# Dividing the gate of the heads' output, instead of the probabilities, by the softmax's row sums

## The chip, the cores and the metric

The program runs on one core of a Trainium2 chip. The metric is the device time of one execution in microseconds. A core has five engines with a queue of instructions each, which run in the order written: TensorE (PE in the profile), VectorE (DVE), ScalarE (ACT), GpSimd (POOL) and SyncE (SP, which only issues DMAs here). They wait for each other through semaphores. TensorE writes its results to PSUM, which the kernel divides into eight banks of 128 partitions by 512 fp32 values; VectorE and ScalarE read them there.

## The reference, cut to what matters

The model has two layers on 512 tokens with 16 learned meta tokens in front (528 rows, width 1024). The first layer mixes by attention with 16 heads of 64, the second by a gated delta net; after each stands a feed-forward block with a short convolution. Only the attention is touched by the change:

```
s = einsum('bhqd,bhkd->bhqk', q_i, k) * scale + c_i[..., :, None] - c[:, :, None, :]
p = softmax(where(mask, s, NEG), axis=-1)
o = einsum('bhqk,bhkd->bhqd', p, v)
o = o * sigmoid(og)
return (o @ w_out)[:, pad:]
```

`c` is the running sum of the log forget gates. The softmax divides each row of exponentials by its sum; the output of each head is then multiplied by a gate.

## The kernel before

Activations lie transposed, features on partitions and tokens along the free axis, in two halves of 272 and 256 tokens. Each fp32 product is made of three passes of rounded parts (hi by hi, hi by lo, lo by hi); `dense` (L312) does this for a weight tile of 1024x128 and one half of the tokens with 24 matmuls. A weight tile comes by DMA, ACT rounds it to its high part (L285), POOL or DVE subtracts to get the low part (L292); six tiles of each part take turns, so L285 waits until the tile used six units earlier has been read.

In attention the loop goes over eight pairs of heads. Each pair has four projections, q, k, v and the output gate og; for each, `push` lets the first half of the tokens run four units ahead of the second. `qk` normalizes q and k (L565 to L592), `vproj` flips v into rows of keys by transposes (L605, L610), and `og` computes the gate SG as exp(-log(1+exp(-z))) in three steps on ACT and one on POOL (L724 to L727), then calls `attend` for its half.

`attend` works on query blocks: 16, 128 and 128 queries in the first half, 128 and 128 in the second. For each block and each of the two heads, `scores` forms the scores in a PSUM bank `sc` (L646 to L649, of which there are two), DVE adds the forget sums and takes the row minimum (L650; signs are turned), ACT exponentiates with the row's sum as a by-product (L653), DVE takes the reciprocal of the sum and multiplies the whole row of probabilities by it (L654, L655). `flip` transposes the probabilities so that keys lie on partitions: first the 16 meta keys of both heads into a PSUM tile `pm` (L666), which ACT copies to PZ (L668) and DVE subtracts to get the low part (L669); then the other keys into tiles `pt` (L678), copied by ACT (L680) and subtracted by DVE (L681). `pm` and all `pt` tiles, those of `vproj` too, take turns in two PSUM banks: an instruction on PE that writes a new tile waits until the readers of the tile before last are done. `values` multiplies with v (L698), adds the parts (L699, L700), multiplies by the gate SG (L701) and rounds (L703, L704).

A flip lags one block behind the scores. The final order on each engine is not the order of the code: a scheduler with a timeline of its own interleaves the attention with the projections of the next pair, and raises those marked with a high priority. Any two instructions on different engines that use the same PSUM bank of one tile are put in order by it, reads included.

Of the kernel before, what the change touches and what calls it, by code (L numbers as in the profile page):

```python
# [9 lines left out]
F32 = mybir.dt.float32  # L10
F32R = mybir.dt.float32r
BF16 = mybir.dt.bfloat16
AF = mybir.ActivationFunctionType
ALU = mybir.AluOpType
# [3 lines left out]
P = 128  # L18
# [7 lines left out]
DH = 64  # L26
# [78 lines left out]
def trunk(ctx, tc, h0, wflat, params, out):  # L105
    nc = tc.nc
# [29 lines left out]
    def psum_tile(kind="ps"):  # L136
        rings = turn["kinds"][kind]
        i = turn.get(kind, 0)
        turn[kind] = i + 1
        ring = rings[i % len(rings)]  # L140
        return psp.tile([P, 512], F32, name=kind, tag=ring, bufs=BANKS[ring])
# [46 lines left out]
    ident = const.tile([P, P], F32, name="ident")  # L188
# [133 lines left out]
    def tmp2(name):  # L322
        return sm.tile([P, 272], F32, name=name, tag="tm2", bufs=5)
# [168 lines left out]
    def attention_heads(layer, OH, OL, cx):  # L492
        ap = cx.enter_context(tc.tile_pool(name="ap", bufs=1, reuse_waits="tile"))
# [15 lines left out]
        def persistent(name, tiles):  # L509
            ring[name] += 1  # L510
            return tiles[ring[name] % 2]
# [34 lines left out]
        for m in range(8):  # L546
            H = {}
# [71 lines left out]
            def attend(half, H=H, m=m):  # L619
                s, n = HALF[half]  # L620
                nkb = 2 if half == 0 else 4
                q0h = 16 if half == 0 else 272
                sfx = "A" if half == 0 else "B"
                Z = []
                PM = persistent("p", PZ)
                for e in range(2):
                    cB = ap.tile([P, s + n], F32, name="cB", tag=f"cB{half}", bufs=2)
                    nc.sync.dma_start(cB[:], cdram[2 * m + e:2 * m + e + 1, 0:s + n].to_broadcast([P, s + n]))
                    PTH = ap.tile([P, nkb, 256], F32R, name="PTH" + sfx, tag="PTH", bufs=2)
                    PTL = ap.tile([P, nkb, 256], F32R, name="PTL" + sfx, tag="PTL", bufs=2)  # L630
                    Z.append((cB, PTH, PTL))

                def scores(e, qb):
                    cB = Z[e][0]
                    QS, QL, KS = H["q", half, e], H["ql", half][e], H["k", e]
                    qs, ql = QB[qb]
                    ke = qs + ql
                    qc = slice(qs - s, qs - s + P)
                    S = ap.tile([P, T], F32, name="S", tag="S", bufs=4)
                    st = ap.tile([P, 4], F32, name="st", tag="st", bufs=6)  # L640
                    segs = ((0, ke),) if ke <= 512 else ((0, 264), (264, 264))
                    for i, (k0, kn) in enumerate(segs):
                        sc = psum_tile("sc")
                        lastseg = k0 + kn == ke
                        o = sc[:, 0:kn]
                        nc.tensor.matmul(o, QS[:, qc], KS[:, k0:k0 + kn], start=True, stop=False)  # L646
                        nc.tensor.matmul(o, QL[:, qc], KS[:, k0:k0 + kn], start=False, stop=not lastseg)
                        if lastseg:
                            nc.tensor.matmul(sc[:, kn - ql:kn], identb[:], cmask[:, :ql], start=False, stop=True)  # L649
                        nc.vector.tensor_tensor_reduce(out=S[:, k0:k0 + kn], in0=o, in1=cB[:, k0:k0 + kn], scale=1.0, scalar=3e38, op0=ALU.add, op1=ALU.min, accum_out=st[:, i:i + 1])  # L650
                    if len(segs) == 2:
                        nc.vector.tensor_tensor(st[:, 0:1], st[:, 0:1], st[:, 1:2], op=ALU.min)
                    nc.scalar.activation(S[:, 0:ke], S[:, 0:ke], AF.Exp, scale=-1.0, bias=st[:, 0:1], accum_out=st[:, 2:3])  # L653
                    nc.vector.reciprocal(st[:, 3:4], st[:, 2:3])  # L654
                    nc.vector.tensor_scalar(S[:, 0:ke], S[:, 0:ke], st[:, 3:4], None, op0=ALU.mult)  # L655
                    if qb == 0:
                        nc.gpsimd.memset(S[:, ke:P], 0.0)
                    return S

                def flip(qb, SS):  # L660
                    qs, ql = QB[qb]
                    qc = slice(qs - s, qs - s + ql)

                    pm = psum_tile("pt")
                    for e in range(2):
                        nc.tensor.transpose(pm[:, e * P:e * P + P], SS[e][:, 0:P], ident[:])  # L666
                    pv = pm[0:NM, 0:2 * P].rearrange("p (e q) -> p e q", e=2)[:, :, 0:ql]
                    nc.scalar.copy(PM[0:NM, :, qc], pv)  # L668
                    nc.vector.tensor_tensor(PM[32:32 + NM, :, qc], pv, PM[0:NM, :, qc].bitcast(F32), op=ALU.subtract)  # L669
                    if qb == 0:  # L670
                        return
                    x0 = qs - q0h
                    for e in range(2):
                        S = SS[e]
                        pt = pm[:, 256:512] if qb == 1 and e == 0 else psum_tile("pt")
                        PTH, PTL = Z[e][1:]
                        for kb in range(1, qb + 1):
                            nc.tensor.transpose(pt[:, (kb - 1) * 128:kb * 128], S[:, QB[kb][0]:QB[kb][0] + 128], ident[:])  # L678
                        pv = pt[:, 0:qb * 128].rearrange("p (k q) -> p k q", q=128)
                        nc.scalar.copy(PTH[:, 0:qb, x0:x0 + 128], pv)  # L680
                        nc.vector.tensor_tensor(PTL[:, 0:qb, x0:x0 + 128], pv, PTH[:, 0:qb, x0:x0 + 128].bitcast(F32), op=ALU.subtract)  # L681


                def values():
                    t = tmp2("avt")
                    w = tmp2("avw")
                    for e in range(2):
                        av = psum_tile("av")
                        PTH, PTL = Z[e][1:]
                        VV = H["v"]  # L690
                        es, eo = slice(64 * e, 64 * e + 64), slice(64 - 64 * e, 128 - 64 * e)
                        mm = [(av[:, 0:n], VV[:, 4, 2 * e:2 * e + 2], PM[:, e, 0:n])]
                        for ptx in (PTH, PTL):
                            for kb in range(1, nkb + 1):
                                lo = max(QB[kb][0], q0h)
                                mm.append((av[:, lo - s:n], VV[:, kb - 1, 2 * e:2 * e + 2], ptx[:, kb - 1, lo - q0h:256]))
                        for i, (o, l, r) in enumerate(mm):
                            nc.tensor.matmul(o, l, r, start=(i == 0), stop=(i == len(mm) - 1))  # L698
                        nc.scalar.copy(w[es, :n], av[eo, 0:n])  # L699
                        nc.vector.tensor_tensor(t[es, :n], av[es, 0:n], w[es, :n], op=ALU.add)  # L700
                    nc.vector.tensor_tensor(t[:, :n], t[:, :n], H["sg", half][:, :n], op=ALU.mult)  # L701
                    oh, ol = OH[half][:, m, :], OL[half][:, m, :]
                    nc.scalar.copy(oh, t[:, :n])  # L703
                    nc.vector.tensor_tensor(ol, t[:, :n], oh.bitcast(F32), op=ALU.subtract)  # L704

                prev = []
                for qb in ((0, 1, 2) if half == 0 else (3, 4)):
                    prev.append((qb, [scores(e, qb) for e in range(2)]))
                    if len(prev) > 1:
                        flip(*prev.pop(0))  # L710
                flip(*prev.pop(0))
                values()

            def og(u, half, H=H, m=m, attend=attend):
                n = HALF[half][1]
                xh, xl, r = xk(half)
                ps = dense(u, half, xh, xl)
                with tc.high_priority(offset=400):
                    z = tmp2("oz")[:, :n]
                    nc.vector.tensor_tensor(z, ps, r[:, :n], op=ALU.mult)  # L720
                    H["sg", half] = ap.tile([P, 272], F32, name="SG", tag="SG", bufs=2)
                    sg = H["sg", half][:, :n]

                    nc.scalar.activation(sg, z, AF.Exp, scale=-1.0)  # L724
                    nc.gpsimd.tensor_scalar(sg, sg, 1.0, 3e38, op0=ALU.add, op1=ALU.min)
                    nc.scalar.activation(sg, sg, AF.Ln)
                    nc.scalar.activation(sg, sg, AF.Exp, scale=-1.0)  # L727
                attend(half)
# [751 lines left out]
```

## Time and profile before

| | |
|---|---|
| median of 3 runs | 1603.53 us (1601.42 to 1608.82) |
| the profiled execution | 1601.35 us, span 1599.4 us |
| busy, share of the span | PE 95%, DVE 70%, ACT 51%, POOL 31% |
| granted TensorE clock | 0.977 in the mean, 1.00 in attention |
| instructions | 33295 |

A page of the profile gives the busy time of each engine, the longest waits and the chain of work that ended last; the trace behind it can be asked for stretches of time, lines and waits. A row of the order of time reads: start, duration, engine, line, operation, tile written and tiles read, shape, count, and in square brackets how long the engine stood idle before it and whose end released it. The durations of matmuls include their latency; successive matmuls overlap, so what one takes of PE is the distance between two starts. A row of stretches gives its length and the busy time of each engine with the number of instructions.

### The profile page before, as it was taken

The page shows a single profiled execution, that of the slowest core. Times are in us where ns is not written, and L with a number is a line of the kernel's source. Part 1 is how long each engine was busy: PE and PEld are TensorE (multiplying, and loading weights), DVE is VectorE, ACT ScalarE, POOL GpSimd, SP SyncE. Part 2 cuts the span into 40 slices and gives each one's busy share as a digit, 9 for nine tenths or more (in the row PEclk, how much of TensorE's full clock was granted, in tenths as well). Part 3 has the DMA queues.
Part 4 walks back from the last instruction along what each step waited for, and adds up shares of the span by engine and source line. Part 5 has one row for each costly group of instructions (what it writes and reads, how often), then busy time and mean ns, then how long its engine had stood idle before and what let it go on. Part 6 is the DMA issues. An engine that isn't in the chain of part 4 may idle for free.

```text
span 1599.4 us, 33295 instructions
## 1 busy us (share of the span) xinstructions
PE 1525.8 (95%) x12630; PEld 1486.8 (93%) x12630; DVE 1123.4 (70%) x2629; ACT 815.4 (51%) x1925; POOL 495.8 (31%) x993
## 2 busy tenths in 40 slices
PE   8999999999999999999789899899989999999996
PEld 6999999899999999999789798898989999999996
DVE  7888888948974675674978665676569864765764
ACT  6677777735643442343564456545456543432441
POOL 6434443025300010012556475654154200100112
PEclk9999999999999999999799998999999999999998
DMA  5232222422223222222323322222141323323321
GB/s 175 89 89 79 75 78 85 134 65 82 84 83 100 93 85 88 93 93 72 107 75 90 90 61 71 68 77 61 50 150 66 91 82 106 92 82 106 93 67 53
DMA packets 63327, 139.04 MB, mean 87 GB/s; under 512 B 18584, under 2 KB 31288, under 8 KB 62784
## 3 DMA queue, kind: packets, MB, share of 16 engines
q1 hardware_dynamic: 62544, 134.55, 28.1%
q8 instruction: 99, 1.62, 0.4%
q0 software_dynamic: 480, 2.15, 0.4%
q14 instruction: 60, 0.49, 0.1%
q10 hardware_dynamic: 144, 0.22, 0.0%
HBM read 131.54 MB, written 5.36 MB: 86 GB/s over the span
## 4 chain that ended last, share of the span: by engine, by line
PE 74%; DVE 11%; POOL 5%; DMA 4%; ACT 3%; issue 3%; SPq 1%; POOLq 0%; DVEq 0%; ACTq 0%
PE ps L312 65%; POOL PR L1177 2%; POOL RB L1178 2%; DVE h L412 1%; DVE bt L411 1%; DVE wl L292 1%; PE av L698 1%; DMA w<-wflat 1%; DVE cv L764 1%; DMA gcr<-gcd 1%; PE pt L678 1%; DVE xl L378 1%; ACT wh L285 1%; PE s L1277 1%; DVE qr L577 1%
## 5 line engine op out<-in xcount | busy, mean ns | idle before, releaser
L312 PE MATMUL ps<-xh,wh 128*128 128x256 f32 (+4 forms) x2464 | 717.6, 293 | 16.8 <-DVE ub L748 9.2
L312 PE MATMUL ps<-xl,wh 128*128 128x256 f32 (+4 forms) x2464 | 710.8, 289 | 3.4 <-DVE xl L378 3.0
L312 PE MATMUL ps<-xh,wl 128*128 128x256 f32 (+4 forms) x2464 | 713.6, 290 | 0.0
L312 PEld LDWEIGHTS ps<-xh,wh 128*128 128x128 f32 (+1 forms) x2464 | 469.6, 192 | 22.8 <-DVE ub L748 6.3
L312 PEld LDWEIGHTS ps<-xl,wh 128*128 128x128 f32 (+1 forms) x2464 | 471.1, 191 | 7.4 <-DVE xl L378 4.6
L312 PEld LDWEIGHTS ps<-xh,wl 128*128 128x128 f32 (+1 forms) x2464 | 471.1, 191 | 1.0
L285 ACT CAST wh<-w 128x1024 fp32r<-128x1024 f32 (+3 forms) x226 | 225.1, 997 | 189.5 <-PE ps L312 166.7
L292 DVE TENSOR_TENSOR wl<-w,wh 128x1024 fp32r<-128x1024 f32 (+4 forms) x191 | 220.6, 1156 | 99.3 <-ACT wh L285 98.7
L764 DVE SCALAR_TENSOR_TENSOR cv<-ub,prm,cv 128x256 f32<-128x256 f32 (+2 forms) x494 | 243.8, 498 | 38.4 <-ACT cv L755 29.5
L312 PE MATMUL ps<-ah,wl 128*128 128x256 f32 (+2 forms) x704 | 199.5, 284 | 0.0
L312 PE MATMUL ps<-ah,wh 128*128 128x256 f32 (+2 forms) x704 | 199.3, 283 | 0.0
L312 PE MATMUL ps<-al,wh 128*128 128x256 f32 (+2 forms) x704 | 199.1, 283 | 0.0
L755 ACT ACTIVATE cv<-ub,prm 128x256 f32<-128x256 f32 (+2 forms) x224 | 113.8, 511 | 146.3 <-DVE ub L748 146.2
L748 DVE TENSOR_TENSOR ub<-ps,r 128x256 f32<-128x256 f32 (+2 forms) x224 | 95.4, 428 | 101.5 <-PE ps L312 100.6
L353 POOL TENSOR_TENSOR ssq<-ssq,sq 128x256 f32<-128x256 f32 (+2 forms) x98 | 90.5, 926 | 144.5 <-ACT sq L352 143.0
L312 PEld LDWEIGHTS ps<-ah,wh 128*128 128x128 f32 x704 | 132.6, 189 | 0.0
L312 PEld LDWEIGHTS ps<-al,wh 128*128 128x128 f32 x704 | 132.5, 188 | 0.0
L312 PEld LDWEIGHTS ps<-ah,wl 128*128 128x128 f32 x704 | 132.4, 188 | 0.0
L751 POOL COPY cy<-ub 128x2 f32<-128x2 f32 (+1 forms) x112 | 38.0, 341 | 279.3 <-DVE ub L748 277.7
L292 POOL TENSOR_TENSOR wl<-w,wh 128x512 fp32r<-128x512 f32 x70 | 95.0, 1377 | 72.1 <-ACT wh L285 56.8
L747 POOL COPY ub<-cy 128x2 f32<-128x2 f32 (+1 forms) x112 | 31.3, 280 | 197.1 <-DVE cv L764 160.0
L786 ACT ACTIVATE gl<-cv 128x272 f32<-128x272 f32 (+2 forms) x88 | 36.7, 418 | 42.0 <-DVE cv L764 41.7
(308 smaller groups left out, 2454.5 us busy)
## 6 DMA issues: line engine op xcount, KB each, us to landing
w<-wflat SPq DMA_DIRECT2D x176, 512.0 KB, 3.5
w<-wflat SPq DMA_DIRECT2D x32, 448.0 KB, 3.3
cB<-cdram SPq DMA_DIRECT2D x16, 264.0 KB, 3.3
w<-wflat SPq DMA_DIRECT2D x16, 256.0 KB, 2.7
h<-h SPq DMA_DIRECT2D x8, 272.0 KB, 5.3
cB<-cdram SPq DMA_DIRECT2D x16, 136.0 KB, 3.0
h<-h SPq DMA_DIRECT2D x8, 256.0 KB, 5.0
AB<-dA SPq DMA_DIRECT2D x16, 128.0 KB, 3.2
```

What stands on the lines that cost most here:

```text
L285: nc.scalar.copy(wh[:], w32)
L292: eng.tensor_tensor(wl[:, c], w32[:, c], wh[:, c].bitcast(F32), op=ALU.subtract)
L312: tok(nc.tensor.matmul(o, w[:, a], r[:, c0:c1], start=(i == 0), stop=(i == tot - 1)))
L353: nc.gpsimd.tensor_tensor(self.acc[:, :n], self.acc[:, :n], sq[:, :n], op=ALU.add)
L747: nc.gpsimd.tensor_copy(ub[:, 0:c0], carry.pop(ft)[:, :c0])
L748: nc.vector.tensor_tensor(ub[:, c0:c0 + n], ps, r[:, :n], op=ALU.mult)
L751: nc.gpsimd.tensor_copy(c[:, :c0], ub[:, n:n + c0])
L755: nc.scalar.activation(cv, ub[:, c0:c0 + n], AF.Identity, scale=w[c0])
L764: nc.vector.scalar_tensor_tensor(cv, ub[:, i:i + n], w[i], cv, op0=ALU.mult, op1=ALU.add)
L786: nc.scalar.activation(g, cv, AF.Gelu_apprx_tanh)
L1177: nc.gpsimd.tensor_tensor(t, R3[:, 0:a, l:l + 1].to_broadcast([P, a, w]), A3[:, l:l + 1, l + 1:32].to_broadcast([P, a, w]), op=ALU.mult)
L1178: nc.gpsimd.tensor_tensor(R3[:, 0:a, l + 1:32], R3[:, 0:a, l + 1:32], t, op=ALU.subtract)
```

## The change

`scores` no longer divides: the exponentials stay as they are, and the sum of each head goes into one column of a small tile `sums`, one for each query block. `flip` takes the reciprocal of both columns at once (L667), POOL spreads them over a 128x128 tile `sb`, 64 columns for each head (L668), PE transposes this into columns 256 to 383 of `pm` (L669), and DVE multiplies the query block's columns of the gate SG by it (L671). As the gate multiplies the heads' output, the division is done there. The tiles `pt` of the second query block no longer share a bank with `pm`. The lines behind move: the meta copy is now L673 and L674, the transposes of the other keys L683, their copies L685 and L686, the product with v L703.

```
-  nc.scalar.activation(S[:, 0:ke], S[:, 0:ke], AF.Exp, scale=-1.0, bias=st[:, 0:1], accum_out=st[:, 2:3])
-  nc.vector.reciprocal(st[:, 3:4], st[:, 2:3])
-  nc.vector.tensor_scalar(S[:, 0:ke], S[:, 0:ke], st[:, 3:4], None, op0=ALU.mult)
+  nc.scalar.activation(S[:, 0:ke], S[:, 0:ke], AF.Exp, scale=-1.0, bias=st[:, 0:1], accum_out=sums[:, e:e + 1])
...
   pm = psum_tile("pt")
   for e in range(2):
       nc.tensor.transpose(pm[:, e * P:e * P + P], SS[e][:, 0:P], ident[:])
+  sb = tmp2("sb")[:, 0:P]
+  nc.vector.reciprocal(sums[:], sums[:])
+  nc.gpsimd.tensor_copy(sb.rearrange("p (e x) -> p e x", e=2), sums[:].unsqueeze(2).to_broadcast([P, 2, DH]))
+  nc.tensor.transpose(pm[:, 256:384], sb, ident[:])
+  sg = H["sg", half][:, qc]
+  nc.vector.tensor_tensor(sg, sg, pm[:, 256:256 + ql], op=ALU.mult)
...
-  pt = pm[:, 256:512] if qb == 1 and e == 0 else psum_tile("pt")
+  pt = psum_tile("pt")
...
+  sums = ap.tile([P, 2], F32, name="sums", tag="sums", bufs=4)
-  prev.append((qb, [scores(e, qb) for e in range(2)]))
+  prev.append((qb, [scores(e, qb, sums) for e in range(2)], sums))
```

The order on ACT around the meta copy of the fourth query block (the first of the second half), before and with the change. PZ0 is the meta tile, pt_2797 and pt_2831 are its `pm`, wh a weight tile's high part, PTHB the copies of the other keys:

```order
L653 ACTIVATE S_2767,st_2768<-S_2767,st_2768 128x528 [waits DVE_49]
L668 CAST PZ0_251<-pt_2797 16x2x128 [waits PE_49]
L653 ACTIVATE S_2782,st_2783<-S_2782,st_2783 128x528 [waits DVE_49]
L680 CAST PTHB_2741<-pt_2802 128x3x128 [waits PE_49]
L653 ACTIVATE S_2902,st_2903<-S_2902,st_2903 128x16 [waits DVE_49]
L726 ACTIVATE SG_2734<-SG_2734 128x256 [waits Pool_49]
L680 CAST PTHB_2745<-pt_2808 128x3x128 [waits PE_49,Activation_49]
L727 ACTIVATE SG_2734<-SG_2734 128x256 [waits Activation_49]
```

```order
L685 CAST PTHB_2781<-pt_2841 128x3x128 [waits PE_49,Activation_49]
L653 ACTIVATE S_2947,sums_2946<-S_2947,st_2948 128x16 [waits DVE_49]
L732 ACTIVATE SG_2774<-SG_2774 128x256 [waits Pool_49]
L733 ACTIVATE SG_2774<-SG_2774 128x256 [waits Activation_49]
L285 CAST wh_3173<-w32_3174 128x1024 [waits DMAHW2_49,PE_49]
L673 CAST PZ0_251<-pt_2831 16x2x128 [waits DVE_49]
L685 CAST PTHB_2785<-pt_2847 128x3x128 [waits PE_49]
```

The meta copy waited for PE and stood ahead of both copies of the other keys; it now waits for DVE (the product with SG) and stands behind the gate's exponentials and a weight cast. On PE, this is what follows the q projection of the second half (ps_3075) that this cast waits for:

```order
L312 MATMUL ps_3075<-xh1_192,wl_2139 128x256
L646 MATMUL sc_2968<-KS_2521,QS_2563 128x144 [waits DVE_49]
L647 MATMUL sc_2968<-KS_2521,QZ10_249 128x144
L649 LDWEIGHTS identb_97
L649 MATMUL sc_2968<-cmask_99,identb_97 128x128
L683 MATMUL pt_2847<-ident_94,S_2796 128x128 [waits DVE_49,PE_49]
L683 MATMUL pt_2847<-ident_94,S_2796 128x128 x2
```

The tile pt_2847 takes the bank of pt_2831. The third place is DVE where the fourth block's scores (sc_2790, sc_2798 for the two heads) are followed by the fifth's (sc_2807, sc_2811, sc_2820), with the change; before it, no reciprocal stood between the fourth block's two score reads and the first of the fifth:

```order
L650 ISA S_2788,st_2789<-sc_2790,cB_2779 128x400 [waits DMAHW3_49,PE_49]
...
L650 ISA S_2796,st_2797<-sc_2798,cB_2783 128x400 [waits DMAHW4_49,PE_49]
...
L671 TENSOR_TENSOR SG_2332<-SG_2332,pt_2426 128x128 [waits PE_49]
L667 RECIPROCAL sums_2787<-sums_2787 128x2 [waits Activation_49]
L650 ISA S_2805,st_2806<-sc_2807,cB_2779 128x264 [waits PE_49]
...
L650 ISA S_2805,st_2806<-sc_2811,cB_2779 128x264
...
L592 TENSOR_TENSOR KS_2521<-qr_2646,KS_2521 64x272 [waits Activation_49]
...
L652 TENSOR_TENSOR st_2806<-st_2806 128x1 [waits DVE_49]
L686 TENSOR_TENSOR PTLA_2340<-pt_2436,PTHA_2339 128x2x128 [waits Activation_49]
L674 TENSOR_TENSOR PZ1_252<-pt_2426,PZ1_252 16x2x128 [waits Activation_49]
L650 ISA S_2818,st_2819<-sc_2820,cB_2783 128x264 [waits PE_49]
```

The reciprocal for both heads now stands between the fourth block's score reads and the fifth's, and the last step of the third block's meta copy (L674, of pt_2426) behind the fifth's first reads. PE's order there is: the third block's transposes, the scores sc_2820 and sc_2824, then the transposes pt_2441, which take the bank of pt_2426.

More of the change, by code (lines that the diff above doesn't have):

```diff
@@ L631, in attend, with scores @@
                     Z.append((cB, PTH, PTL))
-                def scores(e, qb):
+                def scores(e, qb, sums):
                     cB = Z[e][0]
@@ L658, in scores, with flip @@
                     return S
-                def flip(qb, SS):
+                def flip(qb, SS, sums):
                     qs, ql = QB[qb]
```

## Prediction

> **What bounds the kernel now.** I read the stretches of the span first, to see which engine has no room where the change sits.
>
> ```profile
> core 0: us, PE busy (x) PEld busy (x) DVE busy (x) ACT busy (x) POOL busy (x), PEclk, DMA share, GB/s
> 200.00:240.00 40.00, 38.75 (x319) 37.61 (x318) 33.37 (x99) 29.14 (x82) 17.36 (x20) 1.00 0.25 78
> 320.00:360.00 40.00, 38.11 (x308) 37.58 (x307) 19.53 (x39) 15.49 (x33) 8.78 (x12) 1.00 0.22 65
> 520.00:560.00 40.00, 40.00 (x328) 40.00 (x328) 24.90 (x44) 16.55 (x32) 3.32 (x16) 1.00 0.29 93
> ```
>
> Attention runs from about 38 to 340 us. PE is the bound in it, at 38.75 of 40 us, and DVE is not far behind. After it PE is full, so what attention gains or loses in PE time reaches the end nearly one to one. One pair of heads is one period:
>
> ```profile
> 203.64:241.25 37.61, 36.36 (x299) 35.22 (x298) 31.20 (x95) 27.39 (x77) 15.77 (x17) 1.00 0.24 79
> 212.25:241.20 28.95, 28.95 (x246) 28.67 (x245) 24.47 (x80) 20.65 (x59) 12.85 (x15) 1.00 0.27 84
> 203.55:212.25 8.70, 7.45 (x57) 6.59 (x55) 6.76 (x16) 6.74 (x18) 2.92 (x3) 1.00 0.17 63
> ```
>
> PE stands idle 1.25 us of 37.6, all of it in one stretch of 8.7 us in which the third query block is flipped and the next scores begin. Removing every wait there in eight pairs would be worth 10 us; more is not to be had in the steady part. What PE waits for there is in its own order of time:
>
> ```profile
> 208.32 0.44 PE L678 MATMUL pt<-ident,S 128*128 128x128 f32 x2 [0.67 <-DVE PZ L669]
> 211.04 0.39 PE L646 MATMUL sc<-KS,QS 128*128 128x264 f32 x1 [0.56 <-DVE st L650]
> ```
>
> The first is a PSUM bank of the two for `pt` that the meta copy (ACT L668, DVE L669) has not yet given back; the second is a score bank that L650 has not yet read. Neither is the multiplication by the reciprocal. The places to watch are therefore the banks.
>
> **What the change removes and adds.** Per pair DVE loses ten multiplications and ten reciprocals; over the kernel:
>
> ```profile
> L655 DVE TENSOR_SCALAR S<-S,st 128x16 f32<-128x16 f32 (+4 forms) x80 | 30.0, 377 | 1.1
> L654 DVE RECIPROCAL st<-st 128x1 f32<-128x1 f32 x80 | 12.3, 155 | 9.6 <-ACT S L653 9.6
> 218.45 0.28 DVE L617 TENSOR_TENSOR VV<-pt,VV 128x128 fp32r<-128x128 f32 x1
> L609 POOL COPY vm<-vr x8: 287/291/556, 30.4 to 286.3; 128x128 f32<-128x128 f32 x8
> ```
>
> That is 42.3 us of DVE. It gains 40 reciprocals of two columns (as L654, 6.2 us) and 40 products of SG with a PSUM tile (bounds: the 128x128 L617, 0.28 us, and nothing; I take 0.28, 11.2 us): DVE net -25 us. None of this is on PE's path except where PE waits for DVE. POOL gains 40 copies like L609, 11.6 us, with more than half of POOL free. PE gains 40 transposes. Their price is in these rows:
>
> ```profile
> 205.16 0.38 PE L666 MATMUL pt<-ident,S 128*128 128x128 f32 x2
> 205.38 0.38 PE L678 MATMUL pt<-ident,S 128*128 128x128 f32 x2
> 205.51 0.37 PE L312 MATMUL ps<-xh,wl 128*128 128x272 f32 x1
> 205.72 0.29 PE L312 MATMUL ps<-xh,wh 128*128 128x272 f32 x1
> 205.85 0.29 PE L312 MATMUL ps<-xl,wh 128*128 128x272 f32 x1
> ```
>
> Four transposes and one L312 take from 205.16 to 205.72; the L312 is 0.13, so a transpose takes 0.11 us of PE. Five per pair: **+0.55 us**, bounds 0.4 and 0.6.
>
> **What it moves: place one.** The tile `pm` now holds, beside the two flipped meta columns, the flipped sums, and the meta copy on ACT (L673) now waits for DVE's product (L671), which reads the same tile: in ACT's order, as shown ahead for one block, L673 waits for DVE where L668 waited for PE. In the fourth query block of each pair that costs more than the product. ACT's order now has the cast of a weight tile (L285) ahead of L673. This cast waits until PE has finished the q projection of the second half (matmul ps_3075, by wh_2140, six weight tiles earlier in the ring), and one score group later PE has the transpose pt_2847, which needs the bank of pm (pt_2831), so L673 and L674. The prices:
>
> ```profile
> 203.62 1.05 ACT L285 CAST wh<-w 128x1024 fp32r<-128x1024 f32 x1 [0.78 <-PE ps L312]
> 204.57 0.43 ACT L566 ACTIVATE qsq<-qr 128x272 f32<-128x272 f32 x1
> 235.78 0.35 ACT L668 CAST PZ<-pt 16x256 fp32r<-16x256 f32 x1
> 236.16 0.41 DVE L669 TENSOR_TENSOR PZ<-pt,PZ 16x256 fp32r<-16x256 f32 x1 [0.55 <-ACT PZ L668]
> 207.85 0.41 DVE L669 TENSOR_TENSOR PZ<-pt,PZ 16x256 fp32r<-16x256 f32 x1
> 222.98 0.23 PE L646 MATMUL sc<-KS,QS 128*128 128x144 f32 x1
> 223.20 0.36 PE L312 MATMUL ps<-xh,wh 128*128 128x256 f32 x1
> ```
>
> L285 holds ACT 0.95 us (203.62 to 204.57), then L673 0.38 to the start of the subtraction, then 0.41, and 0.06 to PE (as 207.85+0.41 to 208.32 above): 1.80 us after the last reader of the weight tile ends. That end lies 0.28 us behind its issue; PE in the meantime has two matmuls (0.24) and a score group (0.22). The wait: 0.28 + 1.80 - 0.46 = **1.6 us per pair**. Below it lies nothing (if ACT's cast were released earlier); above, some 1.2 us more, one SG addition on POOL (L725, in a row below), if the gate comes late.
>
> **Place two.** In the 8.7 us stretch the scores of the fifth block have moved ahead of the V transposes, and DVE's order has one reciprocal for two heads (L667) ahead of the score reads L650. It waits for both exponentials of the fourth block, and everything behind it on DVE waits too; PE needs the score bank that L650 frees for sc_2820. From the end of the matmul pn_2650 (L573) ACT does, in its order, L575, two L685, L576 and two exponentials:
>
> ```profile
> 208.72 0.49 ACT L575 ACTIVATE qsq<-pn,epst 128x272 f32<-128x272 f32 x1
> 209.10 0.37 ACT L680 CAST PTHA<-pt 128x256 fp32r<-128x256 f32 x1
> 240.03 0.43 ACT L680 CAST PTHA<-pt 128x128 fp32r<-128x128 f32 x2
> 209.35 0.44 ACT L576 ACTIVATE qsq<-qsq 128x272 f32<-128x272 f32 x1
> 211.41 0.63 ACT L653 ACTIVATE S<-S,st 128x400 f32<-128x400 f32 x1
> 211.95 0.19 ACT L653 ACTIVATION_READ_ACCUMULATOR S<-S,st 128x1 f32 x1
> 213.46 0.43 DVE L650 CUSTOM_DVE_ANT_0 S<-sc,cB 128x264 f32<-128x264 f32 x1
> 213.82 0.08 DVE L650 DVE_READ_ACCUMULATOR2_ANT st<- 128x1 f32 x1
> 208.75 0.87 DVE L592 TENSOR_TENSOR KS<-qr,KS 64x256 fp32r<-64x256 f32 x2
> 221.07 0.16 DVE L652 TENSOR_TENSOR st<-st 128x1 f32<-128x1 f32 x1
> 208.30 0.42 DVE L681 TENSOR_TENSOR PTLA<-pt,PTHA 128x256 fp32r<-128x256 f32 x1
> 206.31 1.51 DVE L577 SCALAR_TENSOR_TENSOR qr<-qr,qkg,qsq 128x256 f32<-128x256 f32 x1
> 210.00 0.49 DVE L577 SCALAR_TENSOR_TENSOR qr<-qr,qkg,qsq 128x272 f32<-128x272 f32 x1
> ```
>
> 0.38 + 0.43 + 0.34 (L576 less the 0.1 by which ACT's instructions overlap, as L575 does) + 2 x 0.73 = 2.6, then the reciprocal 0.15, L650 0.43 and hand-overs 0.1: 3.3 us, and 0.28 for the end of the matmul. PE meanwhile issues L573 (0.13), seven transposes (0.77) and the fifth block's score group for the first head (four matmuls at 0.13 and a mask, some 0.6): 1.5. **Wait 2.1 us.** Then DVE has a second L650 (to 0.88 for both, with accumulators), two L592 (0.87), the minimum of two columns (0.15), L686 (0.42) and L674 (0.41) before the bank of pm (pt_2426) is free for pt_2441: 2.7 us from the first L650 on, and 0.5 of that is gone when PE starts; PE has the second head's score group for it, 0.6. **Wait 1.6 us.** Sum 3.7. Bounds: nothing, if the exponentials are done early; and 4.7, if POOL's L292 falls on these DVE steps, since L577 takes 1.51 us beside it and 0.49 without. I stay at the sum of the rows, which are typical ones.
>
> Against it stands the 1.25 us that PE loses now in this stretch, which the new waits contain. Per pair: 0.55 + 1.6 + 3.7 - 1.25 = 4.6 us. The first pair starts behind the forget gates and the last has no next projection, so I take seven pairs: 32 us. On the profiled execution, 1601.35 us (span 1599.4 and 2 us around it), that is 1633.5. This execution lies 2.2 us under the median of the runs shown; I give **1634 us**, between the two readings.
>
> The row behind place one, L673 waiting for DVE, agrees with the Trainium skill, PSUM — Partial Sum Buffer, section "PSUM bank collisions raise a hardware error": reads by ScalarE and VectorE of one bank in the same 32 partitions must not overlap, even in different columns. L671 reads all partitions of pm and L673 the first 16, so by that rule the order is needed; a program without it could copy the meta columns ahead of L671, though the bank would still wait for both. No run here shows such a collision.
>
> **The rivals.** *Cover holds (ends on the other side).* The waits of places one and two exist only if ACT and DVE arrive as late as now. DVE has 25 us less work, 3.1 per pair; if that lets every bank come back in time, the 1.25 us vanish from eight pairs and 0.55 is added: 8 x -0.7 = -5.6, 1596 us. With the idle time at the end of attention (38.11 of 40 above, 1.9 us) and as much at its start gone too, 1592. For it: DVE is at 31.2 of 37.6. Against it: both waits are chains that start from PE itself and run through ACT, whose work is unchanged. It decides if L667 no longer finds L653 unfinished. *Place one alone:* 0.55 + 1.6 - 1.25 = 0.9 x 7 = 6, 1608 us. *The sums come late:* the POOL copies stand behind pairs of L292 and the SG addition, and the transposes of the sums behind them on PE.
>
> ```profile
> 232.86 1.23 POOL L725 TENSOR_SCALAR SG<-SG 128x272 f32<-128x272 f32 x1 [5.10 <-ACT SG L724]
> 235.64 2.56 POOL L292 TENSOR_TENSOR wl<-w,wh 128x512 fp32r<-128x512 f32 x2 [0.55 <-POOL QS L587]
> ```
>
> A whole L292 pair once per pair of heads on top, 2.6 x 8 = 20, gives 1654 us. Against it: in POOL's order the copies stand several microseconds of PE work ahead of their transposes. *It does not do what it says:* the removed instructions are gone from DVE's order, so this has no case of its own.
>
> **How the numbers follow.** Forecast (both places, at between half and 1.4 times their sum: 1616 to 1646) 0.66; the sums late, 1654, 0.12; place one alone, 1608, 0.08; cover holds, 1596, 0.09, or 1592, 0.05. Half a per cent is 8 us, about what this kernel's measurement can tell from no change. Faster by more (under 1595.5): the 1592 case and a part of the 1596 one, 0.07; within: the rest of it and place one alone, 0.15; slower: 0.78. The range leaves out the fastest case and the far part of the late sums: 1600 to 1648.
>
> **What would show it.** Right: in the changed kernel PE waits at L683 for DVE PZ L674 some 1.6 us once per pair, and at L646 and L683 for DVE some 2 and 1.6 us in the stretch of the scores; periods of about 42 us instead of 37.6; PE with some 36.9 busy in each; the time after attention unchanged. Wrong: periods under 38 us; or PE waiting for POOL sb L668, which would put the sums in place of the banks; or a DVE that waits at L667 for nothing.

## The result, and the profile after

The changed kernel takes 1644.45 us (median of 4 runs, 1640.09 to 1645.4) against 1602.47 us for the kernel before on the same chip: a ratio of 1.025, 95% interval 1.0215 to 1.0285. The forecast was 1634 us and slower. The spans of the profiled executions are 1643.4 and 1599.4 us. One execution of e9 below, 1853.18 us at a granted clock of 0.745, was in a slower state and is left out of the time given there.

First, where the time lies. The tile `ub` is written by the first product of the feed-forward block, so its first start (after the durations, first and last start) is taken as the end of attention here; its output projection is in it, which the prediction's 340 us leave out. Before:

```profile
L748 DVE TENSOR_TENSOR ub<-ps,r x224: 401/426/443, 395.6 to 1553.6; 128x256 f32<-128x256 f32 x88, 128x272 f32<-128x272 f32 x14, 128x260 f32<-128x260 f32 x10
```

After:

```profile
L754 DVE TENSOR_TENSOR ub<-ps,r x224: 402/426/445, 434.3 to 1597.3; 128x256 f32<-128x256 f32 x88, 128x272 f32<-128x272 f32 x14, 128x260 f32<-128x260 f32 x10
```

Of the 44 us between the spans, 38.7 have come by the end of attention, and 5.3 after it, where no code differs. The stretch from the start of attention to that point, of the kernel before:

```profile
38.00:395.60 357.60, 344.68 (x2803) 334.11 (x2803) 288.85 (x820) 242.33 (x650) 134.65 (x151) 1.00 0.29 88
```

and of the changed one, with a stretch of one pair of heads:

```profile
38.00:434.30 396.30, 374.63 (x2848) 356.32 (x2847) 269.29 (x742) 240.92 (x650) 142.22 (x191) 0.95 0.26 79
191.00:235.00 44.00, 41.35 (x305) 39.08 (x305) 28.60 (x87) 27.08 (x78) 16.23 (x22) 0.93 0.24 68
```

DVE has lost 19.6 us of work in attention, as meant. PE's idle time (length less busy time) went from 12.9 to 21.7 us. New is the column after the engines: the granted clock was 1.00 and is 0.95. Summed over stretches of 2 us (length times what the clock lacks of 1), that is 18.8 us of clock against 0.0. With 40 transposes of 0.11 us (4.4), 8.8 of idle and 18.8 of clock, 32.0 of the 38.7 us have a place. The other 6.7 count as busy PE, most likely because in a thin stretch a matmul's latency lies under no neighbour. One pair, 305 matmuls, takes about 44 us instead of 37.6; 2.65 of it PE is idle, where it was 1.25.

How the clock falls is seen in stretches of 4 us:

```profile
224.00:228.00 4.00, 3.42 (x27) 2.90 (x25) 3.28 (x5) 1.76 (x6) 2.71 (x2) 1.00 0.00 0
228.00:232.00 4.00, 3.02 (x18) 2.08 (x18) 3.61 (x16) 3.55 (x12) 0.00 (x0) 1.00 0.40 131
232.00:236.00 4.00, 2.71 (x18) 2.22 (x18) 3.73 (x14) 2.56 (x7) 0.00 (x0) 0.88 0.37 93
236.00:240.00 4.00, 4.00 (x27) 4.00 (x26) 1.81 (x6) 1.17 (x3) 0.58 (x2) 0.69 0.19 46
272.00:276.00 4.00, 3.38 (x15) 2.44 (x14) 3.24 (x15) 2.70 (x10) 0.00 (x0) 0.57 0.17 64
276.00:280.00 4.00, 3.41 (x17) 3.26 (x18) 3.09 (x12) 2.31 (x6) 0.10 (x1) 0.50 0.30 100
```

PE issues 18 matmuls in 4 us where a full stretch has 36 (the last row of the next fence); after 8 us of this the clock is 0.5, and the projections that follow run at it until it comes back. Before, one such stretch held 20 matmuls, but only one, and the clock stayed:

```profile
204.00:208.00 4.00, 3.66 (x30) 3.43 (x28) 2.27 (x3) 2.64 (x8) 2.74 (x2) 1.00 0.01 2
208.00:212.00 4.00, 3.09 (x20) 2.46 (x21) 3.88 (x12) 3.56 (x10) 0.00 (x0) 1.00 0.37 133
212.00:216.00 4.00, 4.00 (x36) 3.96 (x36) 3.84 (x15) 2.18 (x8) 0.29 (x1) 1.00 0.01 4
```

What makes PE's stretch thin is in its order of time, after:

```profile
227.52 0.42 PE L646 MATMUL sc<-KS,QS 128*128 128x400 f32 x1 [0.58 <-DVE KS L592]
229.18 0.39 PE L646 MATMUL sc<-KS,QS 128*128 128x264 f32 x1 [0.41 <-DVE st L650]
229.41 0.28 PE L647 MATMUL sc<-KS,QZ 128*128 128x264 f32 x1
...
230.32 0.27 PE L669 MATMUL pt<-ident,sb 128*128 128x128 f32 x1
230.43 0.38 PE L683 MATMUL pt<-ident,S 128*128 128x128 f32 x2
231.39 0.39 PE L646 MATMUL sc<-KS,QS 128*128 128x264 f32 x1 [0.57 <-DVE st L650]
...
233.29 0.41 PE L683 MATMUL pt<-ident,S 128*128 128x128 f32 x2 [0.91 <-DVE PTLA L686]
...
235.45 0.59 PE L703 MATMUL av<-PZ,VV 128*128 128x272 f32 x1 [0.37 <-DVE avt L705]
```

Five waits, 2.84 us, all for DVE, behind four different lines. Between the projection matmul ahead of 227.52 and the next one stand 45 matmuls of attention in PE's order, 22 of them scores: the scores of both blocks of the second half and of the next pair's first block, a flip and both products with v. In the kernel before such a piece has 24, 8 of them scores; the rest is spread between projection matmuls. I call this the *piece* below; it stands once per pair, for six pairs. One pair, cut in two, shows that the time is lost in the piece and right behind it. Before, the piece and then the rest of the pair:

```profile
169.57:174.51 4.94, 3.69 (x25) 2.83 (x24) 4.78 (x13) 3.83 (x10) 0.41 (x2) 1.00 0.31 106
174.51:207.18 32.67, 32.67 (x276) 32.38 (x275) 26.40 (x83) 23.57 (x66) 15.04 (x17) 1.00 0.27 74
```

After:

```profile
182.30:192.99 10.69, 8.07 (x46) 6.12 (x45) 9.31 (x32) 6.11 (x18) 1.26 (x2) 0.89 0.30 95
192.99:226.15 33.16, 33.16 (x259) 32.85 (x259) 19.17 (x53) 20.91 (x58) 15.01 (x21) 0.93 0.22 59
```

(A matmul that straddles a cut is counted on both sides.) In the rest, 259 matmuls take 33.16 us, of which the clock lacks 0.07, or 2.3 us; without that it is 0.119 us for each, as before (32.67 us for 276, 0.118). So nothing else in this pair has become slower.

The waits of PE from 38 to 398 us, after (total, times, longest):

```profile
PE sc L646 <- DVE st L650: 6.1, 13, 0.6
PE pt L683 <- DVE PTLA L686: 4.6, 6, 0.9
PE sc L646 <- DVE KS L592: 4.4, 7, 1.0
PE av L703 <- DVE avt L705: 2.0, 5, 0.9
PE pt L683 <- DVE PZ L674: 0.9, 1, 0.9
```

The wait for L674, on which place one stood, occurs once, not once per pair.

### The profile page after: what moved, and what is told of

Its sections match the earlier page's. It is cut to its first block, busy times and chain, and to the rows that moved or that the text cites. A ratio compares the mean times of both kernels' runs of the same rounds, so it can differ in the third digit from the quotient of the medians.

```text
span 1643.4 us, 33389 instructions
## 1 busy us (share of the span) xinstructions
PE 1560.4 (95%) x12670; PEld 1512.9 (92%) x12670; DVE 1103.9 (67%) x2549; ACT 812.4 (49%) x1925; POOL 501.8 (31%) x1033
## 3 DMA queue, kind: packets, MB, share of 16 engines
q1 hardware_dynamic: 62544, 134.55, 27.3%
## 4 chain that ended last, share of the span: by engine, by line
PE 71%; DVE 11%; POOL 5%; ACT 5%; DMA 4%; issue 3%; SPq 1%; POOLq 0%; DVEq 0%; ACTq 0%
PE ps L312 62%; POOL RB L1184 2%; POOL PR L1183 2%; PE av L703 2%; DVE wl L292 1%; DVE bt L411 1%; DVE h L412 1%; DMA w<-wflat 1%; DMA gcr<-gcd 1%; DVE KS L592 1%; PE pt L683 1%; DVE cv L770 1%; DVE xl L378 1%; ACT wh L285 1%; ACT S L653 1%
## 5 line engine op out<-in xcount | busy, mean ns | idle before, releaser
L312 PE MATMUL ps<-xh,wh 128*128 128x256 f32 (+4 forms) x2464 | 721.5, 295 | 19.6 <-DVE ub L754 11.6
L292 DVE TENSOR_TENSOR wl<-w,wh 128x1024 fp32r<-128x1024 f32 (+4 forms) x191 | 221.8, 1162 | 103.2 <-ACT wh L285 102.6
L292 POOL TENSOR_TENSOR wl<-w,wh 128x512 fp32r<-128x512 f32 x70 | 93.5, 1355 | 46.4 <-ACT wh L285 40.8
```

What stands on the lines that cost most here:

```text
L292: eng.tensor_tensor(wl[:, c], w32[:, c], wh[:, c].bitcast(F32), op=ALU.subtract)
L312: tok(nc.tensor.matmul(o, w[:, a], r[:, c0:c1], start=(i == 0), stop=(i == tot - 1)))
```

## The experiments

Three reasons were to be told apart: the work of the new instructions, the waits for the PSUM bank of `pm` (held longer by the product L671, and by the gate that it waits for), and the order of PE that goes with them.

**e1: without the product.**

```
-  nc.vector.tensor_tensor(sg, sg, pm[:, 256:256 + ql], op=ALU.mult)
```

> The changed kernel without the product of the gate with the flipped sums (L671); the sums, the copy on POOL and the transpose stay, the output is not divided. In the order on PE the longest piece of each pair without a projection falls from 45 matmuls to 24, as before. Theory A (the product, standing ahead of the meta copy, makes the scheduler pack two blocks' scores into one piece without projections, where PE waits and then runs at a lower granted clock): 1595 to 1608 us, clock 1.00 all through attention. Theory B (the 40 transposes and the copies themselves, and waits for POOL, cost the time): at least 1630. Theory C (taking the multiplications off DVE is what moves the order): at least 1630.

Measured: 1602.28 us, ratio 0.9997 (0.9975 to 1.0019). From 38 us to the end of attention:

```profile
38.00:396.50 358.50, 352.53 (x2843) 342.08 (x2842) 262.59 (x699) 243.54 (x650) 149.33 (x191) 0.99 0.27 88
```

The piece has 24 matmuls again. The forty transposes, the POOL copies and their wait are all still there, so none of them is by itself what costs; leaving out one DVE instruction per block, 11 us in all, brings 42 us.

**e2: the kernel before without its division.** The probabilities stay undivided.

```
-  nc.vector.reciprocal(st[:, 3:4], st[:, 2:3])
-  nc.vector.tensor_scalar(S[:, 0:ke], S[:, 0:ke], st[:, 3:4], None, op0=ALU.mult)
```

> The kernel before without the reciprocals and the multiplications of the probabilities, and nothing in their place; the output is not divided. Theory A: 1590 to 1600 us, since of the 1.25 us that PE idles per pair most goes and nothing is added. Theory B: the same. Theory C: 1620 or more, with a lower granted clock in attention.

Measured: 1596.08 us, 0.9956 (0.9935 to 0.9978). 42.3 us of DVE taken away bring 6 to 7 us. As long as the order stays much as it is here, no way of moving the division can win more.

**e3: the product written behind the meta copy.** L671 stands behind L674 in the code, nothing else differs.

> The changed kernel with the product (L671) written behind the meta copy and its subtraction, so that the meta copy waits for PE again and not for DVE; everything else the same. The longest piece without a projection is 37 matmuls instead of 45 (16 of them scores instead of 22). Theory A with the length of the piece as the cause: 1615 to 1635 us, between the two, with a lower clock after the piece. If the wait of the meta copy for the product is the cause by itself: 1600 to 1610.

Measured: 1630.61 us, 1.0163 (1.0129 to 1.0196). The meta copy waits for no product now, though it waits for the transpose of the sums ahead of it (ACT for PE's L669, 10.0 us in 6 waits), and two thirds of the cost stay. The piece has 37 matmuls, 16 of them scores, and the wait is yet another one:

```profile
PE av L703 <- DVE avt L705: 13.6, 12, 1.6
```

So place one of the prediction, the meta copy behind the product, is at most a third of it.

**e4: the sums as in the change, but the probabilities multiplied, in `flip`.** No copy, no transpose, no product:

```
+  nc.vector.reciprocal(sums[:], sums[:])
+  for e in range(2):
+      nc.vector.tensor_scalar(SS[e][:, 0:qs + ql], SS[e][:, 0:qs + ql], sums[:, e:e + 1], None, op0=ALU.mult)
```

> The changed kernel with its sums tile and one reciprocal of two columns per block, but the division put back on the probabilities, two multiplications at the start of each flip; no copy on POOL, no transpose of sums, no product on the gate. No piece without projections over 20 matmuls in most pairs. Theories A and B: 1595 to 1608 us. Theory C does not speak of it. If moving the reciprocal to the flip (one block later in the code) is the cause: 1630 or more.

Measured: 1602.52 us, 0.9998 (0.9981 to 1.0014). A reciprocal that waits for both exponentials, on which place two rested, stands in this kernel too and costs nothing in it.

**e5: the transposed sums in another bank**, the one of the norms `pn`, so that `pm` is as before.

```
+  pz = psum_tile("pn")
-  nc.tensor.transpose(pm[:, 256:384], sb, ident[:])
+  nc.tensor.transpose(pz[:, 0:128], sb, ident[:])
-  nc.vector.tensor_tensor(sg, sg, pm[:, 256:256 + ql], op=ALU.mult)
+  nc.vector.tensor_tensor(sg, sg, pz[:, 0:ql], op=ALU.mult)
```

> The changed kernel with the flipped sums in the one bank that the norms of q and k use, not in the tile of the meta copy; the product reads them there. The meta copy no longer waits for the product. In the order on PE pieces without projections have 22 to 32 matmuls, with at most 6 scores. Theory A (pieces with two blocks' scores are the cost): 1598 to 1612 us, clock 1.00 in attention. If the chain reciprocal, POOL copy, transpose, product is the cost wherever it stands: 1620 to 1645, and waits of PE at the norms' matmuls (L572), whose only bank the product now holds.

Measured: 1626.64 us, 1.013 (1.01 to 1.016). Half of the cost is gone. The longest waits are now ahead of the projections and of the norms, whose bank the sums now use:

```profile
PE ps L312 <- DVE qr L565: 4.6, 7, 1.4
PE pn L572 <- ACT qsq L575: 4.0, 6, 0.7
```

Theory A, the pieces with two blocks' scores, had 1598 to 1612 us here and missed.

**e6 and e7: the sums of all blocks turned at the end of each half, in one tile**, with one product on the heads' output; e6 in the bank of the values `av`, e7 in the bank `pn`.

```
+  pz = psum_tile("av")        # e7: "pn"
+  for qb, sums in allsums:
...
+      nc.tensor.transpose(pz[:, qs - s:qs - s + P], sb, ident[:])
   nc.vector.tensor_tensor(t[:, :n], t[:, :n], H["sg", half][:, :n], op=ALU.mult)
+  nc.vector.tensor_tensor(t[:, :n], t[:, :n], pz[:, :n], op=ALU.mult)
```

> The changed kernel with reciprocal, copy and transpose of the sums moved to the end of a half (one product of 128x272 or 128x256 on the heads' output instead of two or three on the gate), in the one bank of the values. 16 products instead of 40, the 40 transposes stay. Pieces without projections of 21 to 28 matmuls. Theory A: 1598 to 1612 us; the gate's multiplication and the rounding behind it come later, which costs only where the output projection waits for the last half, some 3 us. If the chain is the cost wherever it stands: 1620 or more.

> The same as the run with the values' bank, but with the sums in the bank of the norms. Pieces without projections of 23 or 24 matmuls, nearly none of them scores. Theory A: 1596 to 1610 us. If the chain is the cost wherever it stands: 1620 or more, with waits at the norms' matmuls.

Measured: e6 1614.9 us, 1.0064 (1.0042 to 1.0086); e7 1656.59 us, 1.0325 (1.0299 to 1.0351). The same work differs by 42 us by the bank in which it is put. Theory A misses both, e6 by 3 us (1598 to 1612) and e7 by 47 us (1596 to 1610). In e7 the next norm waits for the heads' output, once for nearly each pair:

```profile
PE pn L572 <- DVE avt L709: 11.3, 7, 1.6
PE av L698 <- DVE avt L700: 8.5, 9, 1.0
```

**e8: no low parts of weights on POOL** in the changed kernel, since L592, two subtractions beside POOL's L292, takes 2.75 us there (224.63) where it took 0.87 before:

```profile
224.38 2.71 POOL L292 TENSOR_TENSOR wl<-w,wh 128x512 fp32r<-128x512 f32 x2 [3.45 <-ACT wh L285]
224.63 2.75 DVE L592 TENSOR_TENSOR KS<-qr,KS 64x256 fp32r<-64x256 f32 x2 [1.00 <-ACT KS L591]
```

```
-LOPOOL = ('attn_w_in',)
+LOPOOL = ()
```

> The changed kernel with all low parts of attention's weights (L292) made on DVE instead of three in four on POOL: some 31 more DVE instructions of 1.16 us, and no POOL work beside DVE's in the piece without projections. The piece is 41 matmuls long. If POOL's work beside DVE's subtraction of K (L592, 2.75 us for two in the changed kernel against 0.87 before) is a cause of its own: 1620 to 1635 us, waits of PE for KS gone. If the length of the piece is all: 1638 to 1655, and the lower clock stays.

Measured: 1648.05 us, 1.0264 (1.0234 to 1.0294) against before: no better than the change. The wait for L592 is nearly gone, others are longer, and the piece still has 41 matmuls:

```profile
PE av L703 <- DVE avt L705: 13.6, 13, 1.6
PE sc L646 <- DVE st L650: 10.7, 15, 1.2
...
PE sc L646 <- DVE KS L592: 1.1, 1, 1.1
```

Here the waits that are named change and the time stays. That turned the question to the order.

**e9: the product without the gate.**

```
-  nc.vector.tensor_tensor(sg, sg, pm[:, 256:256 + ql], op=ALU.mult)
+  rs = tmp2("rs")[:, :ql]
+  nc.vector.tensor_tensor(rs, ident[:, :ql], pm[:, 256:256 + ql], op=ALU.mult)
```

> The DVE product L671 keeps its size and its PSUM operand, but multiplies the transposed sums by a constant tile and writes a tile of its own, so it waits for no gate (the heads' output is not divided in this kernel). If the product costs because it waits for the gate, the exponentials L733 in front of it: as without the product, 1602 to 1606. If it costs because it is one more reader of pm's bank, and orders the meta copy behind it, whatever it waits for: 1630 to 1645, with attention some 25 us or more longer than before and the granted clock below 1 in it. In between: both count.

Measured: 1632.08 us, 1.019 (1.0139 to 1.0242). The gate is not the main thing: without it three quarters of the cost stay.

**e10 and e11: a copy by ACT in place of the product**, in e10 with a product on POOL behind it, in e11 with nothing.

```
-  nc.vector.tensor_tensor(sg, sg, pm[:, 256:256 + ql], op=ALU.mult)
+  rs = tmp2("rs")[:, :ql]
+  nc.scalar.copy(rs, pm[:, 256:256 + ql])
+  nc.gpsimd.tensor_tensor(sg, sg, rs, op=ALU.mult)        # e10 alone
```

> The flipped sums are copied out of pm by ACT, which also makes the meta copy, and POOL multiplies the gate by the copy in SBUF; no DVE instruction waits for the gate, and pm's bank does not wait for it. If the gate is what costs: 1600 to 1608. If any further reader of the bank costs as the product does: 1630 to 1645, and the waits on PE are for the meta copy's last step L676 or the copies of the other keys. If it goes by the length of the stretches in which PE has no projection (32 matmuls here, 45 in the changed kernel, 37 with the product written later, 24 without it): between 1602 and 1631, near 1618.

> ACT copies the flipped sums out of pm as in the run before, and nothing uses them (the heads' output is not divided). What differs from that run is POOL's product alone. If a further reader of the bank costs: as that run or up to 1645 (PE's stretch without projection has 40 to 45 matmuls here). If the gate costs: 1602 to 1606. If the length of that stretch decides: 1635 to 1645.

Measured: e10 1614.29 us, 1.0091 (1.0057 to 1.0125); e11 1632.04 us, 1.0193 (1.0159 to 1.0227). The kernel with *more* work is the faster one by 18 us. The pair differs by one POOL instruction per block and by what the scheduler makes of it: pieces of 32 matmuls, 13 of them scores, in e10, of 37 to 45 with 16 or 22 in e11. By the length of the piece alone e11 had been expected at 1635 to 1645 us; it came out a little faster.

**e12: the order alone.** The kernel before, nothing of the change in it; only the projections of a pair come as q, k, gate, v instead of q, k, v, gate, and v's unit starts attention.

```
-        for s in range(4):
+        for s in (0, 1, 3, 2):
...
-                attend(half)
...
-            push(nextu(), vproj)
             push(nextu(), og)
+            push(nextu(), lambda u, half, f=vproj, a=attend: (f(u, half), a(half)))
```

> The kernel before, with its divided probabilities and no new instruction; only the gate is projected ahead of v, and attention is started by v's unit. This gives PE stretches without projection of 41 matmuls, 22 of them scores, in place of 24 with 8. If such stretches by themselves cost what the change costs: 1622 to 1645, attention 20 to 40 us longer, the granted clock at 0.5 behind some of them. If the cost needs the further reader of pm's bank: 1595 to 1608 and the clock at 1.0 in attention. Between 1608 and 1622 both have a part.

Measured: 1644.85 us, 1.0261 (1.0221 to 1.0301), as slow as the change. Stretches, as for the changed kernel:

```profile
38.00:437.10 399.10, 374.64 (x2804) 359.29 (x2804) 288.48 (x825) 245.11 (x651) 132.07 (x151) 0.93 0.25 79
224.00:228.00 4.00, 3.53 (x27) 2.94 (x26) 2.52 (x9) 3.00 (x8) 2.52 (x2) 1.00 0.00 0
228.00:232.00 4.00, 2.20 (x12) 1.52 (x13) 3.84 (x17) 2.68 (x8) 0.00 (x0) 0.95 0.39 133
232.00:236.00 4.00, 3.71 (x19) 3.51 (x20) 3.44 (x15) 2.59 (x7) 0.00 (x0) 0.50 0.51 111
236.00:240.00 4.00, 4.00 (x26) 4.00 (x26) 1.79 (x5) 1.88 (x6) 2.26 (x2) 0.69 0.10 28
```

DVE and POOL have the work of the kernel before (288.48 and 132.07 against 288.85 and 134.65 us); PE's idle time is 24.5 us and the lost clock 29.0. The piece in these stretches starts at 226.1 us. Inside the piece already the matmuls get longer (0.59 and 0.42 us; the same two shapes take 0.39 and 0.28 in the rows of the changed kernel's trace before its clock falls, as 229.18 there); the wait ahead of them is for a score bank:

```profile
185.65 0.38 PE L678 MATMUL pt<-ident,S 128*128 128x128 f32 x2
187.35 0.59 PE L646 MATMUL sc<-KS,QS 128*128 128x264 f32 x1 [1.31 <-DVE st L650]
187.73 0.42 PE L647 MATMUL sc<-KS,QZ 128*128 128x264 f32 x1
```

The kernels in which `pm` carries the sums, or no bank does, in one table: the piece is counted in PE's order in the steady pairs; attention runs from 38 us to the first `ub`; idle is its length less PE's busy time; lost clock is summed as above.

| kernel | piece: matmuls (scores) | attention us | PE idle us | lost clock us | median us |
|---|---|---|---|---|---|
| before | 24 (8) | 357.6 | 12.9 | 0.0 | 1602.0 to 1604.3 |
| e2, no division | up to 23 (8) | 352.3 | 7.1 | 1.7 | 1596.1 |
| e4, probabilities in `flip` | 19 to 20 (3, 6) | 357.1 | 8.7 | 3.4 | 1602.5 |
| e1, no product | 24 (8) | 358.5 | 6.0 | 3.4 | 1602.3 |
| e10, ACT copy, POOL product | 32 (13) | 365.6 | 10.9 | 1.7 | 1614.3 |
| e11, ACT copy | 37 to 45 (16, 22) | 382.0 | 18.9 | 8.6 | 1632.0 |
| e9, product without gate | 35 to 41 (16, 22) | 385.7 | 22.4 | 8.5 | 1632.1 |
| e3, product later | 37 (16) | 387.7 | 22.0 | 11.9 | 1630.6 |
| the change | 45 (22) | 396.3 | 21.7 | 18.8 | 1644.5 |
| e12, order alone | 41 (22) | 399.1 | 24.5 | 29.0 | 1644.9 |
| e8, low parts on DVE | 41 (22) | 402.9 | 28.8 | 27.3 | 1648.1 |

The time goes with the piece, and above all with the scores in it, but not closely: e11 has 40 matmuls with 22 scores in four of its six pairs, e12 mostly 41 with 22, and they lie 13 us apart. e12 shows that an order with such pieces is enough for the whole cost, without any instruction of the change; what else differs in its order was not taken apart. That the order is also the whole cause in the changed kernel is inferred from the table, from the pair cut in two and from the same falls of the clock, not shown by a run that keeps the change and its short piece. Three kernels that put the sums in other banks don't fit in the table: e5 and e7 have pieces of 22 to 32 matmuls with at most 6 scores, and are slow through other waits, e7 through those for the bank `pn`; their clock falls too (6.8 and 23.9 us lost). e6 has 21 to 30 matmuls with 11 or 16 scores, 14.1 us of idle time and 3.4 of lost clock. What the four slowest (e7, e8, e12 and the change) have in common is a piece that lasts 8 to 12 us by PE's order of time and in which PE waits 1.8 to 3.6 us in all; in e1 it lasts 4.1 us with 0.2 us of waits.

## Why the prediction was right or wrong, step by step

The sign and the range held, and three quarters of the size (31.5 of 42 us); the path to them held in part. That the number came so near is partly luck: one of the two waits in the sum did not come, and the lost clock, which the sum did not have, took its place.

*Transposes, +0.55 us per pair:* right. L669 at 230.32 is followed at 230.43, so 0.11 us each; e1 shows that they cost no more than that.

*DVE net -25 us, off the path:* nearly. The new groups, as the trace lists them (shortest, median and longest ns):

```profile
L671 DVE TENSOR_TENSOR SG<-SG,pt x40: 163/280/291, 48.1 to 369.0; 128x128 f32<-128x128 f32 x32, 128x16 f32<-128x16 f32 x8
L667 DVE RECIPROCAL sums<-sums x40: 95/156/167, 42.7 to 359.4; 128x2 f32<-128x2 f32 x40
L668 POOL COPY sb<-sums x40: 284/293/1063, 43.6 to 361.1; 128x128 f32<-128x128 f32 x40
```

The prices hold (0.28, 0.155 and 0.29 us). DVE is 19.6 us less busy in attention.

*Place one, +1.6 us per pair:* wrong, and the step is "PE has the transpose pt_2847, which needs the bank of pm". It starts before the meta copy has read `pm` at all:

```profile
247.68 0.50 PE L683 MATMUL pt<-ident,S 128*128 128x128 f32 x3
```

```profile
248.46 0.36 ACT L673 CAST PZ<-pt 16x256 fp32r<-16x256 f32 x1
248.85 0.42 DVE L674 TENSOR_TENSOR PZ<-pt,PZ 16x256 fp32r<-16x256 f32 x1 [0.46 <-ACT PZ L673]
```

So it had the other bank; what the section on the change says of the banks of pt_2847 and pt_2441 is wrong. I had read "take turns" as strict alternation in the order of tile numbers; which bank a tile gets must be taken from the waits of the row itself, and one row with a wait for both DVE and PE doesn't name the tile that it waits for.

*Place two, +3.7 us per pair:* right in its place, wrong in its links. The reciprocal doesn't hold DVE up: it starts at 230.84 with no idle time before it, one of the prediction's own signs of being wrong. In e4, too, it is harmless. The transposes pt_2441 wait for L686, not for L674, which has not ended (233.18 + 0.41) when they start at 233.29:

```profile
230.84 0.16 DVE L667 RECIPROCAL sums<-sums 128x2 f32<-128x2 f32 x1
...
233.18 0.41 DVE L674 TENSOR_TENSOR PZ<-pt,PZ 16x256 fp32r<-16x256 f32 x1
```

The five waits come to 2.84 us instead of 3.7.

*Less 1.25 us of old idle time:* right. Per pair the idle time rises by 1.4 us where I had 4.05.

*What was missing:* the granted clock. It makes 18.8 of the 38.7 us, 2.7 for each of my seven pairs (it falls in six), and fills the place of the waits that did not come; hence 44 us per pair instead of the 42 forecast, and PE busy 41 instead of 36.9. I had seen the clock at 1.00 in attention and taken it as given. The Trainium skill describes such falls for another kernel, TensorE: Matmul & The Clock Gate, section "A second HAM failure mode: psum-queue depth-cycling": a PE that pauses briefly and often, because it cycles through PSUM banks, drops to half its clock and recovers, over and over. This case agrees: 0.50 in the stretch from 276 us of the changed kernel, 1.00 all through attention before. By the Trainium skill, same page, section "What's actually happening", the clock had only the values one and one half in three measured kernels, and if so here, the rows between (0.57, 0.69, 0.88) are means over both.

*"The time after attention unchanged":* 1203.8 us before, 1209.1 after (span less first `ub`). Over all the kernels here, with the same code in that part, it lies between 1199 and 1213 us. A part of it may be the clock: among the 24 executions of the kernel before that belong to e1's comparison, the fastest, 1593.94 us, had a mean granted clock of 0.979 and the slowest, 1609.5 us, one of 0.970. What else moves it stays open. In e10 it is 1213.3, so of the 17.5 us between the profiled spans of e10 and before only 8.0 are attention.

*The rivals.* "Cover holds" (1596 or 1592) was nearer for the new work itself (e1 and e4 take as long as the kernel before, though without its gain of 6 us), but not for the order that came with it. "Place one alone" falls with place one. "The sums come late" falls with e1, where the POOL copies and the transposes that wait for them are kept. That the change moves the scores of a whole block between the projections' matmuls could be seen in DVE's order shown ahead of the prediction (the reads of sc_2790 to sc_2820 one behind the other); I priced the instructions there and not the lack of projection matmuls around them.

Left open: why a further reader of `pm` makes the scheduler draw the scores together. Any further reader does it to some degree (e3, e9, e10, e11), while e1 and e4, without one, don't; but e6, which leaves `pm` alone, has 11 or 16 scores in its piece too. That it reckons the bank longer in use and puts the flips later is likely, but was only argued.

No kernel here beats the one before with the division in it.

## What to carry to other kernels

When a scheduler sets the order, count on the engine that bounds the kernel how many dependent instructions stand between two pieces of independent work, before and after: here that ranked the kernels of the table better than any single wait, though it failed where the sums went to another bank (e5, e7). A dependent piece costs twice, by its waits and by the TensorE clock, which fell some 8 us into them in the changed kernel and some 6 us into the piece of e12, and then slows the independent work behind. Ahead of moving work off an engine that is not the bound, take it away altogether once: here that put the gain at 0.4%.

## What the runs showed of the hardware that was not expected

The granted clock halved in stretches where PE was still 68 to 75% busy by the profile (2.71 and 3.02 of 4 us, 18 matmuls each), and came back only within the full stretch behind them (4.00 of 4 us busy, 0.69 in the mean). 4 us with 20 matmuls (3.09 us busy), between stretches with 30 and 36, did not bring it down. POOL's subtraction of low parts and DVE's L592 side by side took DVE 2.75 us for what took 0.87 alone (208.75 in the kernel before, where POOL did nothing from 208 to 212 us), but giving that work to DVE gained nothing (e8).
